# Splitting each unit of weights in one pass of 128x2048 an engine, in an encoder trunk on one core

## The chip, the core and the metric

The kernel runs on one NeuronCore of a Trainium2 chip. The metric is the device time of one execution in microseconds, as the median over runs. The core has TensorE (PE, with its weight loads as PEld), VectorE (DVE), ScalarE (ACT), GpSimd (POOL) and SyncE (SP), which issues nearly all transfers here. Each engine works through its own queue of instructions in a fixed order and waits on semaphores that the others raise.

## The reference

Two identical layers over x of 256 positions by 1024 channels, all in float32:

```
for l in range(DEPTH):                                   # DEPTH = 2
    x = x + 0.5 * swiglu(rms_norm(x), w_gate, w_up, w_down)      # D_FF = 2816
    h = rms_norm(x);  q, k, v, u, g = split(h @ w_in)            # 5 x 512
    a  = dilated_attention(rotary(q), rotary(k), v)              # 8 heads of 64
    sg = gelu(u) * (w_s @ layer_norm(gelu(g)) + b)               # 4 groups, chunks of 128
    x = x + concat(rms_norm(a), rms_norm(sg)) @ w_out
    x = x + 0.5 * swiglu(rms_norm(x), w_gate2, w_up2, w_down2)
return rms_norm(x)
```

`swiglu(h)` is `(silu(h @ w_gate) * (h @ w_up)) @ w_down`. The three dilated windows of the attention are one score matrix with a bias (the logarithm of how many patterns hold a pair), so each head has one softmax over 256 positions.

## The kernel before

All weights are read once, as a stream of 164 units in the order of their use. A unit is up to four blocks of 128x512 side by side: a tile of 128x2048 float32, 1 MB; eight units, the last of each row of `w_down`, have two blocks. To keep float32 precision with the faster matmul format, each unit is split into two parts (`split_unit`, L123 to L134): a high part `whi`, which ScalarE makes by converting `raw` (L133), and a low part `wlo`, which VectorE makes as `raw - whi` (L134). The activations are split in the same way (`xTh`, `xTl`, or two tiles `hT`). Each product of a block then takes three matmuls of 128x512 (L165 to L167; L180 to L182 for the first units): high by high, high by `wlo`, low by `whi`. With two tiles of 128 positions a full unit has 24 matmuls.

`pieces` (L103) says in which pieces a unit is loaded and split. Unit 0 and unit 1 are taken in small pieces, since TensorE waits for them at the start. From unit 2 on a unit is loaded by one transfer, and split in pieces of `size` blocks, here two: `whi` columns 0 to 1023, `wlo` of these, then the same for 1024 to 2047.

There are three buffers each for `raw`, `whi` and `wlo`. `run_ahead` issues loads and splits ahead of the multiplication that uses them: a split is written in program order two units ahead (`AHEAD`), a load up to five. The conversion of a unit must wait for its transfer and for TensorE's last use of the unit three before it, in whose buffer it is put; a transfer waits for the split of the unit three before.

The order in each engine's queue is not that of the source: a scheduler places the instructions by its own estimate of when each could start. So a change of sizes changes the order, too. Around the splits stand, in the feed-forward: on ScalarE the silu (L388, `s`) and one part of the turned products (L279, `hT`); on VectorE the products (L395, `h`), sixteen transposes of 32x256 for each 512 columns (L276, `turned`) and the other part (L280). In the mixer: VectorE adds the bias and takes the maximum of each head's scores (L571, `pr` and `mx`), ScalarE takes the exponentials (L580), VectorE the reciprocal (L582) and the scaling (L583); TensorE transposes the probabilities (`pt`, L596), and ScalarE (L600) and VectorE (L598) copy them out of PSUM to `prT`, every other head each. `attend(a)` and `turn_probs(a)` do four heads. The product with the values (`pav`, L627) and the transposes stand in TensorE's queue between the matmuls of the units of `g` and `u`. Tiles for scores, transposes and `pav` share four banks of PSUM (`ps_sc`).

Of the kernel before, what the change touches and what calls it, by code (L numbers as in the profile page):

```python
# [87 lines left out]
def trunk_kernel(ctx: ExitStack, tc: tile.TileContext, ws, x, cxt, rows, sgw, ident, bias, rot, out):  # L88
# [10 lines left out]
    def f32(ap):  # L99
        return ap.bitcast(F32)  # L100
# [6 lines left out]
    def pieces(i, n, size):  # L107

        if i == 0:
            return [(0, HALF), (HALF, HALF)] + [(c, W) for c in range(W, n * W, W)]  # L110
        step = W if i == 1 else size * W
        return [(c, step) for c in range(0, n * W, step)]
# [11 lines left out]
    def split_unit(i):  # L124
        n = len(UNITS[i][2])
        raw = raws.pop(i)
        hi = wp.tile([P, 4 * W], F32R, tag="whi", name="whi")
        lo = wp.tile([P, 4 * W], F32R, tag="wlo", name="wlo")
        for c, step in pieces(i, n, 2):
            s = slice(c, c + step)  # L130
            if c == 0 and i < 4:
                before(i)
            nc.scalar.activation(hi[:, s], raw[:, s], AF.Copy)  # L133
            nc.vector.tensor_tensor(lo[:, s], raw[:, s], f32(hi[:, s]), op=ALU.subtract)  # L134
        splits[i] = hi, lo
# [3 lines left out]
    def run_ahead(i):  # L139
        while done["load"] < min(len(UNITS), i + AHEAD + RAW_BUFS):  # L140
            load_unit(done["load"])
            done["load"] += 1
            while done["split"] < min(done["load"], i + AHEAD):
                split_unit(done["split"])
                done["split"] += 1
        while done["split"] < min(done["load"], i + AHEAD):
            split_unit(done["split"])
            done["split"] += 1
# [190 lines left out]
    def first_stream():  # L339
        st = Stream(0, 0)  # L340

        warm = act.tile([P, W], BF16, tag="s", name="warm")
        nc.vector.memset(warm, 0.0)
        sink = ps_sc.tile([P, W], F32, tag="sc", name="sink")
        for i in range(WARM):
            nc.tensor.matmul(sink, warm[:, :P], warm, start=True, stop=True)
        nothing = small.tile([P, 1], F32, tag="nothing", name="nothing")
        nc.scalar.activation(nothing, half, AF.Silu)
        for i in range(RAW_BUFS):
            load_unit(i)  # L350
        nonlocal before
        before = st.given
        split_unit(0)
        done["load"], done["split"] = RAW_BUFS, 1
        return st
# [455 lines left out]
```

## Time and profile before

| what | value |
|---|---|
| median of 3 runs | 922.6 us (922.28 to 922.8) |
| the profiled execution | 922.66 us |
| its span, first to last instruction | 920.9 us |
| busy: TensorE / VectorE / ScalarE / GpSimd | 99% / 82% / 51% / 2% |
| mean granted TensorE clock | 0.999 of full speed |
| moved by DMA | 174.14 MB, mean 189 GB/s |

Matmuls are pipelined: a row's duration of 0.39 us for 128x512 overlaps the next one, and the step from one to the next is what counts. A row of the timeline can stand for several equal instructions (x2); its second number is then the time from the first's start to the last's end. The bracket at its end is the idle time of its engine before it, and who ended that.

### The profile page before, as it was taken

What the parts mean: (1) busy time and instruction counts of PE and PEld (TensorE: products, weight loads), DVE (VectorE), ACT (ScalarE), POOL (GpSimd) and SP (SyncE); (2) the same over time, 40 slices, a digit from 0 to 9 for tenths busy, and PEclk for the clock granted to TensorE, in tenths of its full rate; (3) what the DMA queues carried; (4) which work ended last, traced back from release to release, by engine and by line L of the source; (5) the groups of instructions that cost most, each with busy time, mean ns of one, the idle gap of its engine ahead of it and who ended that gap; (6) DMA issues with size and microseconds to landing.
All of it is one profiled execution on the core that took longest, in us unless ns stands there. A gap on an engine that the chain in (4) does not pass through costs nothing.

```text
span 920.9 us, 11064 instructions
## 1 busy us (share of the span) xinstructions
PE 911.0 (99%) x4178; PEld 750.0 (81%) x4178; DVE 752.0 (82%) x1203; ACT 465.5 (51%) x654; POOL 19.4 (2%) x48
## 2 busy tenths in 40 slices
PE   9999999999999999999999999999999999999997
PEld 6888888888788888888888888888887888888886
DVE  6698996697879699896687998966887887998854
ACT  6645444457656544435454444444567545444440
POOL 0000000000000000000000000000000000000000
PEclk9999999999999999999999999999999999999999
DMA  9865556554244546636555555365543455555351
GB/s 328 328 229 183 206 183 230 185 205 180 96 170 170 205 144 214 219 138 245 183 210 174 193 205 201 137 213 220 191 142 127 160 206 183 183 210 200 125 196 47
DMA packets 26982, 174.14 MB, mean 189 GB/s; under 512 B 3120, under 2 KB 4272, under 8 KB 6960
## 3 DMA queue, kind: packets, MB, share of 16 engines
q1 hardware_dynamic: 26496, 172.86, 52.5%
q8 instruction: 33, 0.54, 0.2%
q10 hardware_dynamic: 432, 0.56, 0.2%
q14 instruction: 21, 0.17, 0.0%
HBM read 172.36 MB, written 1.05 MB: 188 GB/s over the span
## 4 chain that ended last, share of the span: by engine, by line
PE 97%; ACT 1%; DVE 1%; issue 0%; DMA 0%; POOL 0%; POOLq 0%; DVEq 0%
PE down L165 8%; PE down L167 8%; PE down L166 8%; PE up L166 7%; PE gate L166 7%; PE gate L165 7%; PE up L165 7%; PE up L167 7%; PE gate L167 7%; PE both L167 2%; PE both L165 2%; PE both L166 2%; PE pav L627 1%; PE g L165 1%; PE oa L165 1%; PE q L167 1%
## 5 line engine op out<-in xcount | busy, mean ns | idle before, releaser
L134 DVE TENSOR_TENSOR wlo<-raw,whi 128x1024 fp32r<-128x1024 f32 (+2 forms) x325 | 378.5, 1202 | 104.4 <-ACT whi L133 102.2
L133 ACT ACTIVATE whi<-raw 128x1024 fp32r<-128x1024 f32 (+2 forms) x325 | 322.6, 1039 | 241.1 <-issue 100.7
L276 DVE STREAM_TRANSPOSE turned<-h 32x256 f32<-32x256 f32 (+1 forms) x384 | 158.9, 414 | 6.3
L166 PE MATMUL down<-wlo,hT 128*128 128x512 f32 x340 | 132.4, 389 | 0.0
L167 PE MATMUL down<-whi,hT 128*128 128x512 f32 x340 | 132.4, 389 | 0.0
L165 PE MATMUL down<-whi,hT 128*128 128x512 f32 x340 | 132.4, 389 | 0.0
L167 PE MATMUL up<-whi,xTl 128*128 128x512 f32 x304 | 118.4, 389 | 0.0
L166 PE MATMUL gate<-wlo,xTh 128*128 128x512 f32 x304 | 118.4, 389 | 0.0
L166 PE MATMUL up<-wlo,xTh 128*128 128x512 f32 x304 | 118.4, 389 | 0.0
L167 PE MATMUL gate<-whi,xTl 128*128 128x512 f32 x304 | 118.4, 389 | 0.0
L165 PE MATMUL up<-whi,xTh 128*128 128x512 f32 x304 | 118.4, 389 | 0.0
L165 PE MATMUL gate<-whi,xTh 128*128 128x512 f32 x304 | 118.2, 389 | 0.0
L167 PEld LDWEIGHTS down<-whi,hT 128*128 128x128 f32 x340 | 63.9, 188 | 13.2
L166 PEld LDWEIGHTS down<-wlo,hT 128*128 128x128 f32 x340 | 63.9, 188 | 13.2
L165 PEld LDWEIGHTS down<-whi,hT 128*128 128x128 f32 x340 | 63.9, 188 | 13.1
L279 ACT ACTIVATE hT<-turned 128x512 fp32r<-128x512 f32 x44 | 26.8, 626 | 80.2 <-DVE turned L276 80.2
L165 PEld LDWEIGHTS gate<-whi,xTh 128*128 128x128 f32 x304 | 57.1, 188 | 11.9
L165 PEld LDWEIGHTS up<-whi,xTh 128*128 128x128 f32 x304 | 57.1, 188 | 11.9
L167 PEld LDWEIGHTS gate<-whi,xTl 128*128 128x128 f32 x304 | 57.1, 188 | 11.8
L167 PEld LDWEIGHTS up<-whi,xTl 128*128 128x128 f32 x304 | 57.1, 188 | 11.8
L166 PEld LDWEIGHTS up<-wlo,xTh 128*128 128x128 f32 x304 | 57.1, 188 | 11.8
L166 PEld LDWEIGHTS gate<-wlo,xTh 128*128 128x128 f32 x304 | 57.1, 188 | 11.7
(172 smaller groups left out, 1059.4 us busy)
## 6 DMA issues: line engine op xcount, KB each, us to landing
raw<-in_ws SPq DMA_DIRECT2D x154, 1024.0 KB, 4.8
raw<-in_ws SPq DMA_DIRECT2D x8, 512.0 KB, 3.2
raw<-in_ws SPq DMA_DIRECT2D x7, 256.0 KB, 5.3
x_sb<-in_x SPq DMA_DIRECT2D x1, 1024.0 KB, 10.8
ln_sb<-in_rows SPq DMA_DIRECT2D x1, 1024.0 KB, 7.5
out<-y SPq DMA_DIRECT2D x2, 320.0 KB, 2.5
xt_sb<-in_cxt SPq DMA_DIRECT2D x1, 512.0 KB, 7.9
sgw_sb<-in_sgw SPq DMA_DIRECT2D x1, 512.0 KB, 6.4
```

Source lines behind the costliest of these rows:

```text
L133: nc.scalar.activation(hi[:, s], raw[:, s], AF.Copy)
L134: nc.vector.tensor_tensor(lo[:, s], raw[:, s], f32(hi[:, s]), op=ALU.subtract)
L165: nc.tensor.matmul(acc[t], xh[:, s], wh, start=start and j == 0, stop=False)
L166: nc.tensor.matmul(acc[t], xh[:, s], wl, start=False, stop=False)
L167: nc.tensor.matmul(acc[t], xl[:, s], wh, start=False, stop=stop and j == len(ks) - 1)
L276: nc.vector.transpose(to[32 * c:32 * c + 32, :, :, b, :], frm[32 * b:32 * b + 32, :, :, c, :])
L279: nc.scalar.activation(dst_hi, src, AF.Copy)
L627: nc.tensor.matmul(bank[j * DH:(j + 1) * DH, p], vs[:, kt, (4 * a + h) * DH:(4 * a + h + 1) * DH], prT[a][:, h, kt], start=kt == 0, stop=k ...
```

## The change

One argument: the split takes its pieces in the size of the whole unit, instead of two blocks. Units 0 and 1 keep their pieces, and so do the units of two blocks. The loads are not touched.

```diff
         hi = wp.tile([P, 4 * W], F32R, tag="whi", name="whi")
         lo = wp.tile([P, 4 * W], F32R, tag="wlo", name="wlo")
-        for c, step in pieces(i, n, 2):
+        for c, step in pieces(i, n, n):
             s = slice(c, c + step)
             if c == 0 and i < 4:
                 before(i)
             nc.scalar.activation(hi[:, s], raw[:, s], AF.Copy)
             nc.vector.tensor_tensor(lo[:, s], raw[:, s], f32(hi[:, s]), op=ALU.subtract)
```

The scheduler moves instructions with it, on ScalarE and VectorE nearly everywhere, on TensorE in units 2 and 3 and at two small products a layer (`ss`). TensorE's queue at unit 2, before (`gate` and `up` are the accumulators, the numbers tell them apart; the first matmul reads `whi` columns 0 to 511):

```order
L180 MATMUL gate_137<-whi,xTh 128x512
L180 MATMUL gate_138<-whi,xTh 128x512
L180 MATMUL up_139<-whi,xTh 128x512
L181 MATMUL gate_137<-wlo,xTh 128x512
L182 MATMUL gate_137<-whi,xTl 128x512
L181 MATMUL gate_138<-wlo,xTh 128x512
L182 MATMUL gate_138<-whi,xTl 128x512
L181 MATMUL up_139<-wlo,xTh 128x512
L182 MATMUL up_139<-whi,xTl 128x512
```

And after:

```order
L180 MATMUL gate_137<-whi,xTh 128x512
L180 MATMUL gate_138<-whi,xTh 128x512
L180 MATMUL up_139<-whi,xTh 128x512
L180 MATMUL up_140<-whi,xTh 128x512
L180 MATMUL gate_141<-whi,xTh 128x512
L180 MATMUL gate_142<-whi,xTh 128x512
L180 MATMUL up_143<-whi,xTh 128x512
L180 MATMUL up_144<-whi,xTh 128x512
L181 MATMUL gate_137<-wlo,xTh 128x512
L182 MATMUL gate_137<-whi,xTl 128x512
```

Before, three products with `whi` came ahead of the first with `wlo`, in steps of half a unit; after, all eight do. Unit 3 has six instead of one.

VectorE's queue in the first mixer, from the last score maximum of the second four heads to the copy (L598) that `pav` waits for, before:

```order
L571 ISA pr,mx<-sc,bias_sb 128x256
L571 ISA mx 128x1
L582 RECIPROCAL sm<-sm 128x4
L583 TENSOR_TENSOR pr<-pr,sm 128x1024
L598 COPY prT<-pt 128x512 x2
L582 RECIPROCAL sm<-sm 128x4
L583 TENSOR_TENSOR pr<-pr,sm 128x1024
L134 TENSOR_TENSOR wlo<-raw,whi 128x1024 x2
L646 BN_STATS st_2003<-vn 128x6 x2
L647 BN_AGGR mv<-st_2003 128x2
L598 COPY prT<-pt 128x512
```

And the same stretch after:

```order
L571 ISA pr,mx<-sc,bias_sb 128x256
L571 ISA mx 128x1
L134 TENSOR_TENSOR wlo<-raw,whi 128x2048
L598 COPY prT<-pt 128x512
L582 RECIPROCAL sm<-sm 128x4
L598 COPY prT<-pt 128x512
L583 TENSOR_TENSOR pr<-pr,sm 128x1024
L646 BN_STATS st_1921<-vn 128x6 x2
L647 BN_AGGR mv<-st_1921 128x2
L598 COPY prT<-pt 128x512
```

The split that stood behind the last scaling (L583) now stands ahead of the two copies, the last reciprocal and that scaling; the scaling of the first position tile (L583) has moved up among the score maxima, and out of this piece.

ScalarE's queue in the same place, as a difference (- before, + after), from the exponentials of the first four heads on:

```order
 L580 ACTIVATE pr,sm<-pr,mx 128x256 x8
-L133 ACTIVATE whi<-raw 128x1024 x2
-L580 ACTIVATE pr,sm<-pr,mx 128x256 x8
-L133 ACTIVATE whi<-raw 128x1024 x2
+L133 ACTIVATE whi<-raw 128x2048
+L580 ACTIVATE pr,sm<-pr,mx 128x256 x4
+L133 ACTIVATE whi<-raw 128x2048
+L600 ACTIVATE prT<-pt 128x512
+L580 ACTIVATE pr,sm<-pr,mx 128x256 x4
+L600 ACTIVATE prT<-pt 128x512
```

The eight exponentials of the second four heads are parted: between them stand a conversion and the first of the copies of `prT`, and the second copy follows. The second mixer has the same order.

## Rows read from the trace of the kernel before

**Rows 1.** The page: busy time of the engines; chain of waits by engine
```profile
PE 911.0 (99%) x4178; PEld 750.0 (81%) x4178; DVE 752.0 (82%) x1203; ACT 465.5 (51%) x654; POOL 19.4 (2%) x48
...
PE 97%; ACT 1%; DVE 1%; issue 0%; DMA 0%; POOL 0%; POOLq 0%; DVEq 0%
```

**Rows 2.** Who TensorE waited for: us in total, times, longest us
```profile
PE pav L627 <- DVE prT L598: 1.7, 2, 0.9
...
PE gate L181 <- DVE wlo L134: 0.2, 1, 0.2
```

**Rows 3.** Groups by line and form: xcount | busy us, mean ns | idle
```profile
L134 DVE TENSOR_TENSOR wlo<-raw,whi 128x1024 fp32r<-128x1024 f32 x316 | 372.9, 1218 | 102.1 <-ACT whi L133 100.0 <-issue 0.2
...
L134 DVE TENSOR_TENSOR wlo<-raw,whi 128x512 fp32r<-128x512 f32 x7 | 4.8, 693 | 2.3 <-ACT whi L133 2.3
...
L133 ACT ACTIVATE whi<-raw 128x1024 fp32r<-128x1024 f32 x316 | 317.3, 1052 | 236.9 <-issue 100.7 <-PE down L167 58.5 <-PE gate L167 30.7
...
L133 ACT ACTIVATE whi<-raw 128x512 fp32r<-128x512 f32 x7 | 4.4, 633 | 2.6 <-DMA raw<-in_ws 2.5
```

**Rows 4.** Timeline of ScalarE, start: start us, us, instruction, [idle before]
```profile
15.09 2.01 ACT L133 ACTIVATE whi<-raw 128x1024 fp32r<-128x1024 f32 x2 [1.81 <-DMA raw<-in_ws]
...
27.72 2.01 ACT L133 ACTIVATE whi<-raw 128x1024 fp32r<-128x1024 f32 x2 [1.73 <-DMA raw<-in_ws]
```

**Rows 5.** Timeline of VectorE, start
```profile
16.18 2.36 DVE L134 TENSOR_TENSOR wlo<-raw,whi 128x1024 fp32r<-128x1024 f32 x2 [2.18 <-ACT whi L133]
...
18.46 1.67 DVE L333 SCALAR_TENSOR_TENSOR xTl<-xt_sb,cols_sb,xTh 128x256 fp32r<-128x256 f32 x4
```

**Rows 6.** Timeline of TensorE, start
```profile
16.66 0.62 PE L180 MATMUL gate<-whi,xTh 128*128 128x512 f32 x2
...
17.46 0.50 PE L181 MATMUL gate<-wlo,xTh 128*128 128x512 f32 x1
...
22.37 0.39 PE L180 MATMUL gate<-whi,xTh 128*128 128x512 f32 x1
...
27.81 0.62 PE L165 MATMUL gate<-whi,xTh 128*128 128x512 f32 x2
```

**Rows 7.** Timeline of TensorE, first mixer
```profile
236.09 1.91 PE L596 MATMUL pt<-id_sb,pr 128*128 128x128 f32 x16
...
244.83 0.39 PE L167 MATMUL u<-whi,xTl 128*128 128x512 f32 x1
...
246.08 1.95 PE L627 MATMUL pav<-prT,v 128*64 128x256 f32 x16 [0.86 <-DVE prT L598]
```

**Rows 8.** Timeline of VectorE, first mixer
```profile
222.10 2.36 DVE L134 TENSOR_TENSOR wlo<-raw,whi 128x1024 fp32r<-128x1024 f32 x2
...
224.38 0.42 DVE L571 CUSTOM_DVE_ANT_0 pr<-sc,bias_sb 128x256 f32<-128x256 f32 x1
...
229.90 0.42 DVE L571 CUSTOM_DVE_ANT_0 pr<-sc,bias_sb 128x256 f32<-128x256 f32 x1 [0.20 <-PE sc L567]
...
232.14 2.36 DVE L134 TENSOR_TENSOR wlo<-raw,whi 128x1024 fp32r<-128x1024 f32 x2
...
234.41 0.42 DVE L571 CUSTOM_DVE_ANT_0 pr<-sc,bias_sb 128x256 f32<-128x256 f32 x1
...
245.36 0.66 DVE L598 COPY prT<-pt 128x512 f32<-128x512 f32 x1
```

**Rows 9.** Timeline of VectorE, first feed-forward, unit 16
```profile
89.32 2.36 DVE L134 TENSOR_TENSOR wlo<-raw,whi 128x1024 fp32r<-128x1024 f32 x2 [0.83 <-ACT whi L133]
```

**Rows 10.** Timeline of TensorE, first feed-forward, unit 16
```profile
93.32 0.39 PE L166 MATMUL gate<-wlo,xTh 128*128 128x512 f32 x1
```

**Rows 11.** Timeline of ScalarE, first mixer
```profile
235.14 0.51 ACT L580 ACTIVATE pr<-pr,mx 128x256 f32<-128x256 f32 x1 [3.04 <-POOL mx L577]
...
239.10 1.99 ACT L133 ACTIVATE whi<-raw 128x1024 fp32r<-128x1024 f32 x2
...
241.00 1.05 ACT L600 ACTIVATE prT<-pt 128x512 f32<-128x512 f32 x2
```

## The prediction

> **What bounds the kernel now.** I read the busy times and the chain that ended last first: TensorE is busy 911.0 of 920.9 us and holds 97% of the chain, VectorE 1% [rows 1]. So the table of who waited for whom matters for TensorE alone. There the reader is to see how little it waits for others: 1.7 us in two places for the copies of transposed probabilities (`prT`), 0.2 us for a low part of weights [rows 2]; what else stands in that table lies ahead of its first product. A change on ScalarE and VectorE can therefore act in two ways only: by moving those few waits, or by making new ones. For new ones I went through the order of instructions, unit by unit, and compared the end of each subtraction with TensorE's first use of it.
>
> The profiled execution took 922.66 us, 920.9 of them span and 1.76 around it; the median of the runs is 922.6. The sum below is added to 922.66.
>
> **What the change removes.** Of the 164 units, 154 go from two pieces to one; units 0 and 1 and the eight of two blocks stay. A conversion of 128x1024 takes 1.052 us and one of 128x512 0.633; a subtraction 1.218 and 0.693 [rows 3]. So 1024 more columns cost ScalarE 2 x 0.419 = 0.84 and VectorE 2 x 0.525 = 1.05, and one piece takes 1.89 us and 2.27 us. Two pieces in a row hold VectorE until the next start for 2.28 us (222.10 to 224.38 in the mixer, the second figure being the next score) [rows 8]; one holds it for about 2.19, since about 0.08 of each duration overlaps the next instruction. The saving, 0.09 x 154 = 14 us of VectorE and some 15 us of ScalarE, lies beside TensorE's work and is worth nothing by itself.
>
> What a unit loses is its overlap: the subtraction starts after 1.89 instead of 1.05 us, so the low part is complete 0.84 - 0.09 = 0.75 us later, and the first halves of both are no longer there early. This costs nothing where the unit is ready ahead of TensorE by more than that. The tightest unit past the first 30 us is number 16: its subtraction starts at 89.32, lasts 2.36, and ends 1.6 us before the matmul at 93.32 that reads it [rows 9, 10]. Every other is ready earlier. Walking the new order through that feed-forward with the durations above (its conversion then stands behind the same transposes, but VectorE has gained on them), unit 16 ends about 3 us ahead of its use. So no cost in the feed-forwards; without that cover a unit would cost up to 0.75.
>
> **The start, a loss of 0.7.** Unit 2 arrives last minute: ScalarE waits 1.81 us for its data and converts from 15.09 [rows 4]; TensorE is there at 16.66, finds the first half converted, does three products with it, and must then wait for the first half of the low part until 17.46 (VectorE 16.18 + 1.22 = 17.40, plus 0.06) [rows 5, 6]. After the change the whole is converted at 15.09 + 1.89 = 16.98, so TensorE starts at 17.04 and not 16.66. A matmul takes 0.227 (24 from 22.37 to 27.81), and 0.11 more when its data came last (0.50 against 0.39) [rows 6]. The new order gives TensorE all eight products of the high part first: 8 x 0.227 + 0.11 = 1.93, to 18.97. The subtraction runs from 17.02 for 2.27 to 19.29, and TensorE goes on at 19.35; sixteen more take 3.74, to 23.09. Before, that was 22.37: **+0.72**. With durations between 1.80 and 2.01 for the conversion, and 2.1 and 2.36 for the subtraction (no slower than two pieces), it is 0.45 to 0.91.
> The delay doesn't grow. Four `xTl` steps follow on VectorE, which began at 18.46 and will begin at 19.2 [rows 5]; the subtraction of unit 3 follows from 20.9 to 23.15, and TensorE wants it only after six products of the high part, at 24.4. Unit 4 was needed at 27.81 and is now at 28.53; ScalarE has no new wait for it. Unit 5 waits for its own transfer anyway (1.73 us, to 27.72) [rows 4], and it is not needed before 33.9.
>
> The Trainium skill speaks against the change here: "Perfetto Trace Analysis", section "Optimizing Scalar/DVE Operations", says that where Scalar and Vector aren't saturated but cause bubbles on other engines, breaking instructions up lets work complete sooner. By that rule a bigger piece costs wherever TensorE waits; the trace agrees for unit 2 alone, since there alone TensorE waits for a split (0.2 us in all), and elsewhere the rule has nothing to act on.
>
> **The mixers, a gain of about 0.5 in each.** TensorE reads in this order: `pt` (first four heads), `u`, `pt` (other heads), `u`, `pav`; before, `pav` started at 246.08 where the last `u` product began at 244.83, so 1.02 us were lost [rows 7], waiting for the copy at 245.36 [rows 8]. That copy stood behind normalization steps, and these behind ScalarE's eight exponentials from 235.14 to 239.10, a conversion to 241.00, and two copies [rows 11]. The new order pulls four exponentials, a conversion and one copy ahead.
> Walking through it: the split at 222.10 ends 0.75 later; 0.28 of that is taken up where VectorE waited for scores at 229.90 (0.20 by the row, the rest a gap beside it), so the fourth score maximum, which now stands ahead of the next split, starts where that split did, at 232.14, plus 0.47: 232.6 instead of 234.41 [rows 8]. Four exponentials then start at 232.6 + (235.14 - 234.41) = 233.3 and, at 3.96 / 8 each, end at 235.3; the conversion behind them ends at 237.2, and only then ScalarE copies the first head, to 237.7. The fourth head's transposes now need the bank that this copy frees, where before they needed a score maximum: TensorE would reach them at 236.09 + 12 x 0.104 = 237.3 (sixteen take 1.66) [rows 7] and waits **0.43**. On VectorE the split starts at 232.95, two maxima, a reciprocal, a third maximum, the 1.14 us scaling, two maxima, the next split 237.8 to 239.95, a copy, a reciprocal, a copy and the last scaling follow, to 242.45. TensorE, 0.43 late, wants that scaling at 242.46: a wait of about **0.1**. ScalarE's normalization inputs are done by 242.6 and 243.2, and the copy that `pav` wants ends near 244.6, ahead of TensorE's arrival at 245.06 + 0.53 = 245.6. The old wait of 1.02 is gone: 1.02 - 0.53 = 0.5 gained. Layer 1 has the same order, and its wait was as long [rows 2], so **-1.0** in all.
> The bounds: at best no new wait comes, -2.04. At worst VectorE's chain is later than I have it; each 0.1 us of that reaches TensorE at the last scaling, and one further split in front (2.2) makes 2.2 - 0.5 = +1.7 a layer, +3.4.
>
> Behind `pav`, the square sums (`ss`) move one block of products back on TensorE and their inputs are ready 0.5 us before; the transition to the second feed-forward has its last `xTl` done at about 280.1, TensorE there at 280.2 and needing it 4 us later. Nothing is added there. The eight small units and the tail after the last unit are unchanged.
>
> **Sum:** 922.66 + 0.72 - 1.0 = **922.4**. Its own range, from the two terms half-way to their bounds, is 921.4 to 923.6.
>
> **Rivals.**
> 1. Slower: VectorE's queue in the mixer. The last scaling has no slack in my walk, so this is the place. If the chain of scores comes more than 0.5 us later, the gain is used up and each layer loses; with one whole split ahead of the chain, the time is 922.66 + 0.72 + 3.4 = 926.8. For it: the copies now stand behind a 2.27 us instruction. Against it: the maxima and exponentials start 1.8 us earlier. Chance 0.12.
> 2. Faster: VectorE is the hidden bound, and grouping frees it. VectorE is 82% busy [rows 1], and up to 14 us are saved. Against it: TensorE waits for VectorE 1.9 us in all past its first matmul [rows 2], so no more can be won: with both `prT` waits gone and the start free, 922.66 - 2.04 = 920.6. Chance 0.07.
> The same section of the Trainium skill has this as a rule: larger operations improve throughput if the engine is saturated. By that rule the time would be at the 920.6 of this rival; the trace shows TensorE as the saturated one.
> 3. Nothing reaches TensorE: the start's loss is hidden by an earlier landing and the mixers' waits stay as they are: 922.6. For it: 97% of the chain is TensorE at a steady step. Against it: at 15.09 ScalarE takes unit 2 up without slack. Chance 0.15.
>
> **How the numbers follow.** My forecast has 0.66. About 0.2%, 1.8 us, is what a measurement tells from no change: same is 920.8 to 924.4. The forecast and rival 3 lie within it (0.81); rival 1 makes slower 0.12 and rival 2 faster 0.07. The range reaches half-way into rival 1, 921.0 to 924.8, and leaves out 920.6 and the worst of rival 1.
>
> **What would show it.** In the profile after: conversions of 128x2048 at about 1.89 us and subtractions at 2.27; TensorE's first matmul of unit 2 at 17.0 and unit 3 at 23.1; `pav` without a wait of 0.9 for `prT`, and `pt` with a new one for ScalarE's `prT` of about 0.4; no wait of TensorE for `wlo` or `whi` past 30 us. I am wrong if such waits appear in the feed-forwards, or if `pt` waits over 1 us a layer.

## The result: 7.7 us slower, and the profile after

The changed kernel takes 930.16 us (median of 4 runs, 929.87 to 930.31), the kernel before 922.45 us beside it: a ratio of 1.0082, 95% interval 1.007 to 1.0094. That is 0.8% slower. The forecast was 922.4, the range 921.0 to 924.8; the time lies 5.4 us above its upper end. The profiled execution took 930.12 us, 928.3 of them span.

The page of the changed kernel, busy times and chain, answers to [rows 1]:

```profile
PE 912.3 (98%) x4178; PEld 748.7 (81%) x4178; DVE 742.3 (80%) x1049; ACT 453.3 (49%) x500; POOL 33.6 (4%) x48
...
PE 87%; DVE 6%; ACT 3%; DMA 1%; issue 1%; POOL 1%; SPq 0%; POOLq 0%
```

VectorE and ScalarE are busy for 10 and 12 us less (14 and 15 were forecast), and TensorE for 912 where it was 911. But TensorE now holds 87% of the chain instead of 97%, VectorE 6% instead of 1%. GpSimd is busy for 33.6 us where it was 19.4, with the same 48 instructions. This is the key to the result.

Who TensorE waited for in the changed kernel (us in total, times, longest), against [rows 2]:

```profile
PE pt L596 <- DVE pr L583: 3.1, 2, 1.6
PE pt L596 <- ACT prT L600: 2.2, 2, 1.1
PE pt L596 <- DVE mx L571: 1.8, 2, 0.9
...
PE q L167 <- DVE xTl L323: 0.8, 2, 0.4
```

The wait of `pav` is gone, as forecast. In its place there are three waits of `pt` in each mixer, 1.6 + 1.1 + 0.9 us, and a wait of `q`. Where the 7.4 us of span went is read from the start of some units on TensorE, in the two timelines:

| unit, and what lies before it | before | after | difference | new |
|---|---|---|---|---|
| 3: the start | 22.37 | 23.01 | +0.64 | +0.64 |
| 36: the first feed-forward | 196.45 | 197.09 | +0.64 | 0 |
| 38: the first block products of the mixer (`q`) | 207.46 | 208.66 | +1.20 | +0.56 |
| 42: projections, first scores | 234.72 | 235.96 | +1.24 | +0.04 |
| 46: the rest of the mixer | 268.88 | 272.92 | +4.04 | +2.80 |
| 116: two feed-forwards | 639.74 | 643.79 | +4.05 | 0 |
| 120: `q` of layer 1 | 661.61 | 666.24 | +4.63 | +0.58 |
| 128: the mixer of layer 1 | 723.01 | 730.46 | +7.45 | +2.82 |
| 162, computed together with 163: the last feed-forward | 906.19 | 913.64 | +7.45 | 0 |

So the feed-forwards cost nothing, the start 0.6 in these two profiles, each `q` 0.6 and each mixer 2.8.

**The mixer.** VectorE in the first mixer of the changed kernel, from the fourth maximum (L571) of the first position tile on, for the second four heads:

```profile
233.85 0.41 DVE L571 CUSTOM_DVE_ANT_0 pr<-sc,bias_sb 128x256 f32<-128x256 f32 x1
...
234.19 2.28 DVE L134 TENSOR_TENSOR wlo<-raw,whi 128x2048 fp32r<-128x2048 f32 x1
236.40 0.41 DVE L571 CUSTOM_DVE_ANT_0 pr<-sc,bias_sb 128x256 f32<-128x256 f32 x1
...
238.68 0.18 DVE L582 RECIPROCAL sm<-sm 128x4 f32<-128x4 f32 x1 [1.86 <-ACT pr L580]
...
240.91 2.29 DVE L134 TENSOR_TENSOR wlo<-raw,whi 128x2048 fp32r<-128x2048 f32 x1
...
245.40 0.18 DVE L582 RECIPROCAL sm<-sm 128x4 f32<-128x4 f32 x1 [1.60 <-ACT pr L580]
...
246.07 1.21 DVE L583 TENSOR_TENSOR pr<-pr,sm 128x1024 f32<-128x1024 f32 x1
```

GpSimd there:

```profile
227.92 0.19 POOL L577 TENSOR_SCALAR mx<-mx 128x4 f32<-128x4 f32 x1 [35.20 <-DVE mx L571]
229.30 0.19 POOL L577 TENSOR_SCALAR mx<-mx 128x4 f32<-128x4 f32 x1 [1.19 <-DVE mx L571]
234.35 2.17 POOL L577 TENSOR_SCALAR mx<-mx 128x4 f32<-128x4 f32 x1 [4.86 <-DVE mx L571]
241.08 2.17 POOL L577 TENSOR_SCALAR mx<-mx 128x4 f32<-128x4 f32 x1 [4.55 <-DVE mx L571]
```

ScalarE there:

```profile
236.56 0.51 ACT L580 ACTIVATE pr<-pr,mx 128x256 f32<-128x256 f32 x1 [2.56 <-POOL mx L577]
...
240.35 0.57 ACT L600 ACTIVATE prT<-pt 128x512 f32<-128x512 f32 x1
243.29 0.51 ACT L580 ACTIVATE pr<-pr,mx 128x256 f32<-128x256 f32 x1 [2.36 <-POOL mx L577]
```

TensorE there:

```profile
239.23 0.66 PE L596 MATMUL pt<-id_sb,pr 128*128 128x128 f32 x4 [0.86 <-DVE mx L571]
240.98 0.66 PE L596 MATMUL pt<-id_sb,pr 128*128 128x128 f32 x4 [1.10 <-ACT prT L600]
...
247.43 1.83 PE L596 MATMUL pt<-id_sb,pr 128*128 128x128 f32 x15 [1.59 <-DVE pr L583]
...
250.57 1.95 PE L627 MATMUL pav<-prT,v 128*64 128x256 f32 x16
```

Between the maximum and the exponential stands one small instruction that I had passed over: GpSimd turns the sign of the maximum (L577, 128x4). At 227.92, beside a maximum on VectorE, and at 229.30, beside none, it takes 0.19 us. At 234.35 and at 241.08 it takes 2.17, and ends at 236.52 and 243.25, 0.05 us after the subtractions that VectorE had begun at 234.19 and 240.91 (ends 236.47 and 243.20). ScalarE's exponentials start right behind it, at 236.56 and 243.29, with 2.56 and 2.36 us idle before. The second mixer has the same two rows of 2.17. The rest follows: VectorE's reciprocal waits 1.86 us for the first of them, with the other maxima queued behind it (TensorE's `pt` waits 0.86 for these); ScalarE's copy of the first head stands behind a conversion and comes at 240.35 (1.10); the last scaling comes at 246.07 (1.59). These three are 3.55 us, the old wait of `pav` was 0.86 [rows 7]: 2.69 of the 2.80.

The negations grouped, first in the changed kernel, then in the kernel before:

```profile
L577 POOL TENSOR_SCALAR mx<-mx 128x4 f32<-128x4 f32 x8 | 9.5, 1183 | 91.6 <-DVE mx L571 91.6
```

```profile
L577 POOL TENSOR_SCALAR mx<-mx 128x4 f32<-128x4 f32 x8 | 1.5, 193 | 88.7 <-DVE mx L571 88.7
```

Four of the eight were held, so the mean is 1183 ns where it was 193.

**The start.** TensorE at units 2 and 3, VectorE and ScalarE, against [rows 4, 5, 6]:

```profile
16.74 0.39 PE L182 MATMUL up<-whi,xTl 128*128 128x512 f32 x1
16.96 0.68 PE L180 MATMUL gate<-whi,xTh 128*128 128x512 f32 x2
...
19.24 0.50 PE L181 MATMUL gate<-wlo,xTh 128*128 128x512 f32 x1 [0.23 <-DVE wlo L134]
...
23.01 0.62 PE L180 MATMUL gate<-whi,xTh 128*128 128x512 f32 x2
```

```profile
16.90 2.29 DVE L134 TENSOR_TENSOR wlo<-raw,whi 128x2048 fp32r<-128x2048 f32 x1 [3.07 <-ACT whi L133]
```

```profile
14.95 1.92 ACT L133 ACTIVATE whi<-raw 128x2048 fp32r<-128x2048 f32 x1 [1.85 <-DMA raw<-in_ws]
```

The high part is whole at 16.87. TensorE starts unit 2 at 16.96, one step behind its last product of unit 1 and without a wait; it waits for the low part once and starts unit 3 at 23.01. Of the 0.64, 0.30 was there when unit 2 began (16.96 against 16.66): unit 1, whose code didn't change, had started 0.30 later as well (11.52 against 11.22). The other 0.34 arose within unit 2. Experiment 4 takes the moment at which the data landed out of this.

**The wait of `q`.** VectorE at the end of the first feed-forward, before and after (the subtraction at which VectorE had last waited, and the first use of what `q` needs):

```profile
184.14 2.36 DVE L134 TENSOR_TENSOR wlo<-raw,whi 128x1024 fp32r<-128x1024 f32 x2 [3.03 <-ACT whi L133]
...
201.78 1.67 DVE L323 SCALAR_TENSOR_TENSOR xTl<-turned,cols_sb,xTh 128x256 fp32r<-128x256 f32 x4
```

```profile
185.64 2.29 DVE L134 TENSOR_TENSOR wlo<-raw,whi 128x2048 fp32r<-128x2048 f32 x1 [3.10 <-ACT whi L133]
...
203.00 1.67 DVE L323 SCALAR_TENSOR_TENSOR xTl<-turned,cols_sb,xTh 128x256 fp32r<-128x256 f32 x4
```

TensorE, after:

```profile
203.54 0.50 PE L167 MATMUL q<-whi,xTl 128*128 128x512 f32 x1 [0.40 <-DVE xTl L323]
```

The high part of the unit comes 0.64 later as TensorE does, and its whole instead of half is 0.86 more: VectorE begins 1.50 later. From there to `xTl` it has no idle time in which to regain it; only the four passes up to there are 0.28 shorter together. `xTl` comes 1.22 later, TensorE only 0.64, and had no slack.

### The profile page after: what moved, and what is told of

Its sections match the earlier page's. It is cut to its first block, busy times and chain, and to the rows that moved or that the text cites. A ratio compares the mean times of both kernels' runs of the same rounds, so it can differ in the third digit from the quotient of the medians.

```text
span 928.3 us, 10752 instructions
## 1 busy us (share of the span) xinstructions
PE 912.3 (98%) x4178; PEld 748.7 (81%) x4178; DVE 742.3 (80%) x1049; ACT 453.3 (49%) x500; POOL 33.6 (4%) x48
## 4 chain that ended last, share of the span: by engine, by line
PE 87%; DVE 6%; ACT 3%; DMA 1%; issue 1%; POOL 1%; SPq 0%; POOLq 0%
PE down L167 8%; PE down L166 8%; PE down L165 8%; PE gate L165 7%; PE up L165 7%; PE gate L167 7%; PE up L167 7%; PE up L166 7%; PE gate L166 7%; DVE wlo L134 2%; PE both L167 2%; PE both L166 2%; PE both L165 2%; ACT whi L133 1%; DVE turned L276 1%
## 5 line engine op out<-in xcount | busy, mean ns | idle before, releaser
L134 DVE TENSOR_TENSOR wlo<-raw,whi 128x2048 fp32r<-128x2048 f32 (+2 forms) x171 | 367.8, 2153 | 125.9 <-ACT whi L133 123.5
L133 ACT ACTIVATE whi<-raw 128x2048 fp32r<-128x2048 f32 (+2 forms) x171 | 308.4, 1804 | 260.7 <-PE down L167 79.5
```

## The experiments

Each ran beside the kernel before on the same chip. `chain([...])` below adds edges that fix the order in which an engine's queue takes instructions, without any wait; the keys name an instruction (`mx` a maximum, `rc` reciprocal, `sc` scaling, `cp` copy to `prT`, `hi` and `lo` the high and the low part of a unit's split).

Theory A: the subtraction, with both inputs in SBUF, holds GpSimd off for its whole length, and GpSimd stands in the path from scores to probabilities. Rival B: the new order on VectorE and ScalarE makes the loss by itself. Rival C: whole pieces are simply late for the mixer. The loss of a mixer below is the time from the start of unit 42 to that of unit 46 (124 to 128 in layer 1), against the kernel before: 2.80 and 2.85 us in the changed kernel.

**1. neg_on_act: the order kept, the negation taken off GpSimd.**

```diff
-nc.gpsimd.tensor_scalar(mx[:, t, 1, s], mx[:, t, 0, s], -1.0, 0.0, op0=ALU.mult, op1=ALU.add)
+nc.scalar.activation(mx[:, t, 1, s], mx[:, t, 0, s], AF.Copy, scale=-1.0)
+chain(order of the changed kernel on VectorE); chain(the same on ScalarE)
```

> The changed kernel with the order of every instruction on VectorE and TensorE held fixed as it is there; only the negation of the score maxima (L577, eight in all) goes from GpSimd to ScalarE, just ahead of its exponentials. Theory A (a GpSimd instruction stands still while VectorE runs a subtraction with two SBUF inputs): the third and fourth negation no longer take 2.17 us but some 0.2, the exponentials of the second four heads start about 2.0 us earlier for the first position tile and about 4.0 for the second, and TensorE's three waits for pt (3.5 us a layer) shrink to about 0.5; time 922.9 to 924.3, likeliest 923.2. Rival B (the order alone, the reciprocal and the scaling between the maxima and the copies behind a whole pass): unchanged, 929.8 to 930.5. Rival C (bigger pieces are late for the mixer as such): unchanged, too.

Measured 925.58 us (ratio 1.0031, 1.0019 to 1.0042): 4.6 us back. The mixers now lose 0.43 and 0.55. So B and C fall as the cause of the loss: with the same order and the same pieces most of it is gone, and what is left is the most that they can be worth. The size was missed, by 1.3 us from the range's end: TensorE's waits for `pt` shrank to 1.4 us a layer, not to 0.5. TensorE's waits and two rows of ScalarE show the rest:

```profile
PE pt L596 <- ACT prT L600: 2.0, 2, 1.0
...
PE pt L596 <- DVE mx L571: 0.7, 2, 0.4
```

```profile
227.95 0.21 ACT L577 ACTIVATE mx<-mx 128x4 f32<-128x4 f32 x1 [3.74 <-DVE mx L571]
228.18 1.28 ACT L580 ACT_TABLE_LOAD   x1
```

The load of the exponential's table, which ScalarE did while it was idle (at 224.16 in the changed kernel), now stands behind the negation and waits with it: the first exponential starts at 229.47 instead of 228.15. That is a cost of this experiment's edit; how much of the 0.43 and 0.55 it makes, and how much the order, this run doesn't tell.

**2. halves_new_order: the order kept up to the statistics, GpSimd kept, the passes halved.**

```diff
-for c, step in pieces(i, n, n):
+for c, step in pieces(i, n, 2 if i % 82 in range(41, 46) else n):
+chain(order of the changed kernel on VectorE, up to the statistics); chain(ScalarE)
```

> The changed kernel with the order of the mixers' scores, scalings and copies held fixed as it is there, but units 41 to 45 of each layer split in two pieces of 128x1024; the negation on GpSimd. Theory A, held for one instruction: the third and fourth negation take about 1.0 us instead of 2.17, and the mixers lose about half; 925 to 927.5, likeliest 926.3. Theory A, held over both passes that follow one another: they take 2.2 us and the time stays at 929.5 to 930.5. Rival B: 929.5 to 930.5 with negations at any length.

Measured 925.54 us (1.003, 1.002 to 1.004), within the range. GpSimd, and the two subtractions beside the first of its long negations:

```profile
233.41 1.11 POOL L577 TENSOR_SCALAR mx<-mx 128x4 f32<-128x4 f32 x1 [5.18 <-DVE mx L571]
239.07 1.10 POOL L577 TENSOR_SCALAR mx<-mx 128x4 f32<-128x4 f32 x1 [4.55 <-DVE mx L571]
```

```profile
233.24 2.36 DVE L134 TENSOR_TENSOR wlo<-raw,whi 128x1024 fp32r<-128x1024 f32 x2
```

The negation now takes 1.11 us: from 233.41 to 234.52, when the first of the two subtractions is over (233.24 + 1.2), though the second follows at once. GpSimd is held for one instruction, so the length of a single pass sets the delay. The mixers lose 0.51 us each, less than the half that I had expected: a delay half as long on GpSimd is not half the loss on TensorE. This run halves the pieces, too, so against rival C it proves less than neg_on_act.

**3. old_order: whole pieces and GpSimd kept, the order of before.**

```diff
+chain([lo 42, mx x8, rc, sc, mx, mx, rc, mx, sc, lo 43, mx x5, rc, sc, cp 1, cp 3, rc, sc, lo 44])
+chain([hi 42, exp x16 with hi 43 between the first and second eight, hi 44, cp 0, cp 2])
```

> The changed kernel, all pieces whole, the negation on GpSimd; in the mixers the order on VectorE and ScalarE held to that of the kernel before (all maxima of the second position tile together, the subtraction ahead of the last five of them, so that none stands right behind a fourth maximum). Theory A: the negations take 0.19 us, TensorE's three waits for pt are gone, the wait of pav for prT comes back at 1.3 to 1.6 us (0.9 before); time 924.5 to 926.5, likeliest 925.5. Rival B: the same, since the order is the old one. Rival C (whole pieces are late for the mixer as such): 929 to 930.5.

Measured 923.32 us (1.0009, 0.9999 to 1.0018), below the range. The negations and TensorE's longest wait past the start:

```profile
L577 POOL TENSOR_SCALAR mx<-mx 128x4 f32<-128x4 f32 x8 | 1.5, 193 | 89.6 <-DVE mx L571 89.6
```

```profile
PE ss L665 <- DVE sq L659: 1.6, 2, 0.8
```

No subtraction stands beside a negation, and all eight take 0.19. The mixers take 0.47 and 0.40 us less than in the kernel before; what is left of the loss lies at the start and at `q`. I had expected the wait of `pav` back; it didn't come, since the scheduler now put the copy (L598) whose bank `pav` needs ahead of the normalization's statistics (L646). A new wait of `ss` (0.8) took up part of that gain: sums of squares behind the split of unit 46.

**4. two_pieces_edges.** Edit: `pieces(i, n, 2 if i == 2 or i % 82 in range(34, 39) else n)`.

> The changed kernel with two pieces for unit 2 and for units 34 to 38 of each layer, which are split at the end of the first feed-forward and in the first product of the mixer; the mixers' order as after. If the start's loss is the whole high part of unit 2, unit 3 starts at 22.4 again instead of 23.0 (-0.64); if TensorE's wait for xTl at q (0.56 a layer) comes from these units' subtraction starting 0.85 later in VectorE's queue, it goes (-1.1): 928.2 to 928.8, likeliest 928.4. If that wait comes from the inverse root on GpSimd (1.40 instead of 0.94 us there), it stays: 929.5.

Measured 928.37 us (1.0058, 1.0043 to 1.0073), as forecast. The waits of `q` are gone. That alone doesn't rule out GpSimd's sum (L263): just before `q` it is back at 0.94 us here, where the changed kernel has 1.40. The changed kernel's own timeline does: `xTl` (L323) reads nothing that comes from this sum, and between 185.64 and 203.00 VectorE goes from one instruction to the next with no gap over 0.03 us.

Unit 3 started at 21.87, 1.14 earlier than in the changed kernel, which is more than the edit is worth. In the twelve profiles of this study the conversion of unit 2, which waits for its transfer, begins anywhere from 14.46 to 15.35. Counted from there, unit 3 starts after 8.06 to 8.09 us in the four profiles with a whole unit 2, and after 7.27 to 7.38 in the eight others (7.28 here). So a whole unit 2 costs 0.77 us in the mean, whenever its data lands.

**5. ffn_whole and mixer_whole: is the ledger complete?** Edits: `pieces(i, n, 2 if i == 2 or i % 82 in range(34, 47) else n)`, and `pieces(i, n, n if i % 82 in range(41, 47) else 2)`.

> The changed kernel with two pieces wherever its trace showed a loss: unit 2, units 34 to 38 (end of the first feed-forward and first product of the mixer) and 41 to 46 (mixer) of each layer; whole pieces everywhere else, which is in the feed-forwards. If the ledger of the loss is complete (start +0.64, xTl at q +0.56 twice, mixers +2.84 twice), it is back at the time of before: 922.0 to 923.1, likeliest 922.5, though VectorE and ScalarE are each some 10 us less busy than before. Rival (VectorE's saved time is worth something in the feed-forwards): 920 to 921.5.

> The kernel before with whole pieces for units 41 to 46 of each layer alone (12 of 164). Theory A with the order that the scheduler then makes (a pass right behind the last maximum of each position tile): the third and fourth negation take 2.17 us, TensorE waits three times for pt in each mixer, +2.8 twice: 927.7 to 928.7, likeliest 928.2. Rival (the loss in the mixers is left by lateness that builds up in the feed-forward's whole pieces): 922 to 924.

Measured 922.64 us (1.0003, 0.9994 to 1.0012) and 928.65 us (1.0066, 1.0053 to 1.008), both as forecast. Whole pieces in the feed-forwards alone take the load of VectorE from 752.0 to 744.2 us and change nothing; twelve whole units in the mixers alone bring 6.2 of the 7.7 us, with negations of 1184 ns in the mean again.

**6. pinned_whole, pinned_halves, pinned_halves2: a version that beats both, and whether size matters.** Whole pieces but for unit 2 and units 34 to 38, the order of experiment 3, and these pins:

```diff
+chain([..., "lo 44", "cp of the second four heads, 1", "bn_stats 0"])      # VectorE
+chain(["sums L658, L659", "lo 46"]); chain(["square L635 of the second pav", "hi 46"])
+chain([..., "bn_stats 0", "bn_stats 1", "bn_aggr 0", "cp ..., 3", "bn_aggr 1", "lo 45"])   # pinned_halves2
```

> A version meant to beat both: whole pieces, but two for unit 2 and units 34 to 38; in the mixers the order of before (no subtraction behind a fourth maximum), and three pins more: the copy of prT that frees the bank for pav goes ahead of the normalization's statistics, and the square of pav and the sums of squares (L635, L658, L659) go ahead of the split of unit 46. Expected: no wait of pt, pav, ss or q; the start as before (within 0.4), each mixer 1.0 to 1.4 us shorter than before: 919.6 to 921.0, likeliest 920.1. If the ss wait (0.8 a layer) only moves elsewhere: 921.7.

> The kernel before, two pieces of every unit, with the same pins as pinned_whole in the mixers. If the order of the copy ahead of the statistics is what gains and the size of the pieces is worth nothing: within 0.4 of pinned_whole, 919.8 to 920.8, likeliest 920.4. If the whole pieces are worth something by themselves: 921.5 or more.

Measured 919.68 us (0.997, 0.9959 to 0.9982) for whole pieces, and 921.94 us (0.9993, 0.9984 to 1.0002) for halves with the same pins, which by the expectation would make whole pieces worth 2 us. But the two don't have the same order, as VectorE and TensorE of pinned_whole and TensorE of pinned_halves show:

```profile
241.80 2.28 DVE L134 TENSOR_TENSOR wlo<-raw,whi 128x2048 fp32r<-128x2048 f32 x1
244.00 0.68 DVE L598 COPY prT<-pt 128x512 f32<-128x512 f32 x1
244.64 1.29 DVE L646 BATCH_NORM_STATS2 st<-vn 128x6 f32<-128x512 f32 x2
```

```profile
245.16 1.95 PE L627 MATMUL pav<-prT,v 128*64 128x256 f32 x16
```

```profile
252.34 1.08 PE L627 MATMUL pav<-prT,v 128*64 128x256 f32 x6 [0.53 <-DVE prT L598]
```

In pinned_whole the copy at 244.00 comes ahead of the statistics, `pav` starts without a wait, and each mixer is 1.5 us shorter than before. In pinned_halves the scheduler had put half a subtraction ahead of the next copy, and `pav` waits 0.53 in its middle. With that copy pinned as well, both have the same order on VectorE from the scores to the sums of squares, and the same on TensorE:

> As pinned_halves, all units in two pieces, and with the second copy of prT that pav waits for (the fourth head's) pinned ahead of the split of unit 45, as it stands in pinned_whole, so that both have the same order on VectorE and TensorE in the mixer. If the size of the pieces is worth nothing: no pav wait, each mixer 1.4 to 1.6 us shorter than before, 919.4 to 920.2, likeliest 919.7. If whole pieces are worth something by themselves: 920.7 or more.

> The same kernel as pinned_whole, run beside pinned_halves2 on the same chip, so that the two can be compared: 919.7 again, within 0.4.

Measured 919.56 us (0.997, 0.9957 to 0.9982) for halves, 919.79 us (0.9973, 0.9963 to 0.9984) for whole pieces. The two differ by 0.2 us, less than the runs of one of them do (918.91 to 920.78). So the gain of 2.7 to 2.9 us comes from the order of the mixers, and with that held the size of the pieces (but at the start and at `q`, where both have two) is worth nothing that these runs can tell.

## Why the prediction was wrong, step by step

- **What bounds the kernel; the saving is worth nothing by itself.** Right: ffn_whole.
- **Durations.** Right. Expected were 1.89 and 2.27 us, and 2.19 from pass to next start; the groups of the changed kernel show 1.914 and 2.290, and from 234.19 to 236.40 it is 2.21:

```profile
L134 DVE TENSOR_TENSOR wlo<-raw,whi 128x2048 fp32r<-128x2048 f32 x154 | 352.7, 2290 | 119.5 <-ACT whi L133 117.1
L133 ACT ACTIVATE whi<-raw 128x2048 fp32r<-128x2048 f32 x154 | 294.6, 1914 | 245.1 <-PE down L167 74.7 <-PE up L167 54.2 <-issue 47.1
```

- **The start, +0.72.** The size and what sets it are right: from the start of unit 2's conversion TensorE goes on with the low part after 4.29 us (14.95 to 19.24; 4.26 forecast), and counted from there the loss is 0.77. The wait for the whole high part was not seen: TensorE came 0.09 us after it was done. That it started unit 2 at 16.96, so near the forecast 17.04, and unit 3 at 23.01 (23.09), is in part luck, since it came 0.30 late from unit 1.
- **No cost in the feed-forwards.** Right for their units (unit 16 has its low part at 90.93, 3.0 us ahead of its use at 93.96, as forecast), and wrong at their end. I held the end of each subtraction against TensorE's first use of that unit, and didn't ask what else stands behind the late subtraction in VectorE's queue. There it was `xTl`, which TensorE took without slack: 0.57 a layer, 1.14 in all.
- **The mixers, -0.5 each.** This is the step that failed. The walk held up to the fourth maximum: forecast for 232.6, with the 1.24 us that TensorE is later by then 233.84, and it started at 233.85. The next sentence, "Four exponentials then start at 232.6 + (235.14 - 234.41) = 233.3", took the distance from the maximum to the exponential from a row in which no subtraction ran beside GpSimd's negation. In the new order one starts right behind the maximum, and the distance was 2.71 us instead of 0.73. The same happened at the second position tile. So `pt` waited 1.10 us for ScalarE's copy where 0.43 was forecast, 1.59 for the last scaling where 0.1 was, and 0.86 for a maximum where nothing was: 3.55 a layer, over the 1 us that was named as the sign of being wrong. neg_on_act and halves_new_order show that it is this instruction: 2.4 and 2.3 us of the two mixers' loss go when it leaves GpSimd, and beside a pass of half the size it takes 1.11 us instead of 2.17.
- **Rival 1** had the place and the sign, not the mechanism: what came late was not VectorE's queue but GpSimd beside it, and the price of 1.7 a layer was 1.1 too low. Its chance of 0.12 was too small for a walk that left the last scaling no slack.
- **The bounds** took in one delay of a pass in each mixer; there were two of 2.0 us, one for each position tile, and nothing stood there for `q`. The sum's own range was worked out wrongly besides: half-way from 0.72 to 0.45 and 0.91, and from -1.0 to -2.04 and +3.4, gives 921.7 to 924.7, not 921.4 to 923.6. The result lies outside both.

The trace of before had the clue, in an engine that I had not opened because it is busy for 2%. GpSimd's first sum of the mixer (L263) took 0.94 us there and 0.20 at the start, and it ended at 190.02, right behind the second of two subtractions beside it (187.62 to 189.97):

```profile
23.98 0.20 POOL L263 TENSOR_TENSOR root<-ssq 128x2 f32<-128x2 f32 x1 [23.14 <-ACT junk L257]
...
189.08 0.94 POOL L263 TENSOR_TENSOR root<-ssq 128x2 f32<-128x2 f32 x1 [163.85 <-ACT junk L257]
```

```profile
187.62 2.35 DVE L134 TENSOR_TENSOR wlo<-raw,whi 128x1024 fp32r<-128x1024 f32 x2
```

The Trainium skill states the rule, in "SBUF — State Buffer", sections "SBUF: two separate sides" and "Who interferes with whom": a VectorE instruction with two SBUF inputs takes its second through the read interface that GpSimd shares, and against a GpSimd instruction that reads SBUF whichever came first blocks the other for its whole length. The trace agrees: 2.17 us beside a subtraction of 2.29, 1.11 beside one of half that size, 0.19 beside a maximum (L571, at 227.92), whose scores come from PSUM. By that rule a larger operation on VectorE is also a longer block for GpSimd, and that is what this change paid for.

## What to carry to other kernels

Follow a chain through every engine that it touches, also one that is busy for 2%: a small GpSimd instruction between two others costs its own 0.2 us, or the rest of the VectorE pass with two inputs in SBUF that happens to stand beside it (2.17 us here). When an instruction gets larger, ask what stands behind it in its queue and beside it on the engine that shares its way to memory, not only who reads its result. And where a scheduler reorders with every edit, compare two sizes with the order held; here the order was worth 8.5 us with the same pieces (two_pieces_edges 5.7 slower than the kernel before beside it, pinned_whole 2.8 faster), and the size nothing measurable with the same order.

## What the runs showed of the hardware

A held GpSimd instruction ends 0.05 us after VectorE's does (236.52 against 236.47), and is released between two subtractions that follow one another (1.11 us, not 2.3; halves_new_order). The instruction's busy time in the trace contains the block: a GpSimd row that is ten times as long as its like (2.17 against 0.19) is a wait, though it isn't listed as one and TensorE's table of waits names VectorE and ScalarE only. ScalarE's table load (1.28 us) waits with an instruction that is queued ahead of it, and then no longer hides in idle time (neg_on_act).
